# The halo of a causal convolution summed by ScalarE, and a ratio with two scalar factors, in a two-layer mLSTM and differential-attention trunk

## The chip, the core and the metric

The program runs on one core of a Trainium2 chip. The metric is device microseconds of one execution, as the median of three runs. In every text here PE is TensorE (PEld its weight loads), DVE is VectorE, ACT is ScalarE, POOL is GpSimd, and SP is the engine that issues the DMAs.

## What is computed

Two layers over 2048 positions of width 1024. Each layer normalises its input, multiplies it by one wide matrix, and gives the columns to four mLSTM heads and four differential-attention heads. The two places that the change touches are the causal convolution of the mLSTM's q and k columns, and the factor with which the second attention map is subtracted from the first:

```python
def causal_conv(x, w, b):          # w: 4 taps per channel
    y = lax.conv_general_dilated(x, w..., padding=[(K - 1, 0)], feature_group_count=C)
    return y + b
...
    qk = jax.nn.silu(causal_conv(jnp.concatenate([mq, mk], -1), conv_w, conv_b))
    mq_c, mk_c = jnp.split(qk, 2, axis=-1)
    hm = mlstm_chunkwise(to_heads(mq_c), to_heads(mk_c), to_heads(mv), mi + i_bias, mf + f_bias)
...
        p = jax.nn.softmax(jnp.where(mask, s, -jnp.inf), axis=-1)
        a = p[:, :, 0] - lam * p[:, :, 1]
        return jnp.einsum('bhqk,bhke->bhqe', a, vt)
```

## The kernel before, in words

Positions are cut into four time blocks of T = 512 (index `t`), heads into four units (`u`), each with one mLSTM head and one attention head. So there are 2 x 4 x 4 = 32 units of work. In each, PE projects the unit's columns: a group of 24 matmuls for one 128-column piece fills one PSUM tile `mm` (three buffers in all) with channels on the partitions and the 512 positions along the free dimension. Matrices are split into a high and a low part (`wh`, `wl`; `hth`, `htl`) and three products are summed. ACT makes `wh` from each loaded piece (L194), POOL makes `wl` (L196).

For the q piece and the k piece (`qk` = 0 and 1) the function `post` in `proj_conv` does the convolution; that is 64 convolutions in all. ACT writes the last tap and the bias into `cacc` (L406). DVE then adds three taps from PSUM, shifted by 1, 2 and 3 positions (L410). The first 1, 2 or 3 positions of a block need the last three positions of the block before it, the halo: a small tile of 128 x 3 kept from there. After each tap a second, small DVE instruction adds the halo's part of that tap (L412). Then ACT copies this block's last three positions into the halo tile (L414), and `silu2` follows: ACT's tanh of `cacc` (L394), and a DVE product (L395).

For attention, DVE takes the scores from PSUM into SBUF with their row maximum (L735), ACT takes the exponent with its sum (L679). When both maps of a query block are there, `ratio` sums the parts (`zz`, L687), takes the reciprocal of the second map's sum (L692) and multiplies it by the first map's sum and by `nl`, minus lambda (L693). `chunk` adds the second map, scaled by that, to the first (L699). PE transposes the result into `tpa`; ACT takes the high part of it (`ath`, L801), DVE the low part (`atl`, L802), and PE multiplies both with the values (`pv`). PE needs `ath` for the first of these products and `atl` for the second.

The code puts all this into one list of tasks with due times; each task emits its instructions, and a scheduler with a timeline of its own then sorts them into one queue for each engine. TensorE's tasks are held in the order of their streams by extra dependencies. So any change of an instruction can change the order of others in a queue. Each engine works through its queue in order.

Of the kernel before, what the change touches and what calls it, by code (L numbers as in the profile page):

```python
# [12 lines left out]
F32 = mybir.dt.float32  # L13
F32R = mybir.dt.float32r
BF16 = mybir.dt.bfloat16
AF = mybir.ActivationFunctionType
ALU = mybir.AluOpType
AX = mybir.AxisListType

P = 128  # L20
S = 2048
D = 1024
T = 512
# [29 lines left out]
def trunk_kernel(ctx, tc, x, w_ch, w_v0, w_v, w_o, nw, cw, cb, gb, mnw, msk, anw, lam,  # L53
                 fnw, rope, out, n_layers=NL, n_t=NT):
    nc = tc.nc
    V, A, G, PE, SY = nc.vector, nc.scalar, nc.gpsimd, nc.tensor, nc.sync

    cp = ctx.enter_context(tc.tile_pool(name="cp", bufs=1))
# [9 lines left out]
    def st(shape, tag, dt=F32, name=None):  # L68
        return sb.tile(shape, dt, tag=tag, name=name or tag, bufs=BUFS[tag])

    def sm(cols, name):
        return sb.tile([P, cols], F32, tag="s_" + name, name=name, bufs={"mx": 2, "zc": 2, "nm": 2, "s12": 4}.get(name, 1))
# [14 lines left out]
    def after(r, name):  # L87
        tc.add_manual_dep(r.ins, name, nosync, reason="TensorE order")
# [42 lines left out]
    def behind(r):  # L131

        if "r" in first:
            after(r, first["r"])
        return r

    def params(l):
        pr = par[l]
        for nm, src, w in (("cw", cw[l], 32), ("cb", cb[l], 8),
                           ("mnw", mnw[l], NH), ("msk", msk[l], NH), ("anw", anw[l], 1)):  # L140
            t_ = cp.tile([P, w], F32, tag=f"{nm}{l}", name=f"{nm}{l}")
            SY.dma_start(t_, src)
            pr[nm] = t_
        t_ = cp.tile([P, 8], F32, tag=f"gb{l}", name=f"gb{l}")
        SY.dma_start(t_, gb[l].partition_broadcast(P))
        pr["gb"] = t_
        lt = st([P, 4, 64], "tmp", name="lam")
        SY.dma_start(lt, lam[l].partition_broadcast(P))
        lam_init = 0.8 - 0.6 * math.exp(-0.3 * l)
        lp = st([P, 2, 64], "tmp", name="lp")  # L150
        behind(V.tensor_tensor(lp[:, 0], lt[:, 0], lt[:, 1], op=ALU.mult))
        behind(V.tensor_tensor(lp[:, 1], lt[:, 2], lt[:, 3], op=ALU.mult))
        ls = cp.tile([P, 4], F32, tag=f"ls{l}", name=f"ls{l}")
        V.tensor_reduce(out=ls[:, 0:2], in_=lp, axis=AX.X, op=ALU.add)
        A.activation(ls[:, 2:4], ls[:, 0:2], AF.Exp)
        nl = cp.tile([P, 1], F32, tag=f"nl{l}", name=f"nl{l}")

        V.tensor_tensor(nl, ls[:, 3:4], ls[:, 2:3], op=ALU.subtract)
        V.tensor_scalar(out=nl, in0=nl, scalar1=-lam_init, scalar2=None, op0=ALU.add)
        pr["nl"] = nl  # L160

        behind(V.tensor_scalar(out=pr["anw"], in0=pr["anw"], scalar1=(1.0 - lam_init), scalar2=0.5,
                               op0=ALU.mult, op1=ALU.mult))
        behind(V.tensor_scalar(out=pr["mnw"], in0=pr["mnw"], scalar1=0.5, scalar2=None, op0=ALU.mult))
        behind(V.tensor_scalar(out=pr["msk"], in0=pr["msk"], scalar1=0.25, scalar2=None, op0=ALU.mult))

        for h in range(NH):
            hq = cp.tile([P, 2, 3], F32, tag=f"halo{l}{h}", name=f"halo{l}{h}")
            G.memset(hq, 0.0)
            pr["halo"].append(hq)  # L170
        mc = cp.tile([1, NH], F32, tag=f"mc{l}", name=f"mc{l}")
        G.memset(mc, 0.0)
        pr["mc"] = mc
# [121 lines left out]
    def proj_ch(l, u, g, H, post):  # L295

        c = {}

        def hi(dc):
            def f():  # L300
                half, j = divmod(dc, 4)
                if dc == 0:
                    c["ps"] = pst("mm", [P, T])
                if j == 0:
                    c["w"] = load_w(w_ch[l, u, g, half], 512)
                w = c["w"][0][:, j * P:(j + 1) * P]
                mm(c["ps"], w, H["hh"][dc], dc == 0, False)
                mm(c["ps"], w, H["hl"][dc], False, False)
            return f

        def lo(d0):
            def f():
                for dc in (d0, d0 + 1):
                    j = dc % 4
                    mm(c["ps"], c["w"][1][:, j * P:(j + 1) * P], H["hh"][dc], False, dc == 7)
                if d0 == 6:
                    post(c["ps"])
            return f

        return [(0.44, f) for half in range(2)  # L320
                for f in [hi(4 * half + j) for j in range(4)] + [lo(4 * half + j) for j in (0, 2)]]
# [69 lines left out]
    def silu2(dst, src):  # L391

        th = st([P, T], "tmp", name="th")
        A.activation(th, src, AF.Tanh, scale=0.5)  # L394
        V.scalar_tensor_tensor(out=dst, in0=th, scalar=1.0, in1=src, op0=ALU.add, op1=ALU.mult)  # L395

    def proj_conv(l, u, qk, H, X):

        pr = par[l]

        def post(ps):
            halo = pr["halo"][u]
            ch = qk * NH + u
            w = lambda j: pr["cw"][:, ch * 4 + j:ch * 4 + j + 1]
            acc = st([P, T], "tmp", name="cacc")
            A.activation(acc, ps, AF.Identity, scale=w(3), bias=pr["cb"][:, ch:ch + 1])  # L406
            for j in (2, 1, 0):

                d = 3 - j
                V.scalar_tensor_tensor(out=acc[:, d:], in0=ps[:, 0:T - d], scalar=w(j), in1=acc[:, d:],  # L410
                                       op0=ALU.mult, op1=ALU.add)
                V.scalar_tensor_tensor(out=acc[:, 0:d], in0=halo[:, qk, j:3], scalar=w(j), in1=acc[:, 0:d],  # L412
                                       op0=ALU.mult, op1=ALU.add)
            A.activation(halo[:, qk], ps[:, T - 3:T], AF.Copy)  # L414
            nm = "mq" if qk == 0 else "mk"
            X[nm] = st([P, T], nm)
            silu2(X[nm], acc)

        return proj_ch(l, u, qk, H, post)
# [244 lines left out]
    def scores(l, t, u, X, pair):  # L664

        pr = par[l]
# [17 lines left out]
        def ratio(qi, cq, r=None):  # L684
            zz = X["zz"]
            qb = 2 * pair + qi
            z_ = V.tensor_reduce(out=zz[:, qb], in_=cq["zc"][:, :, 0:t + 1], axis=AX.X, op=ALU.add)  # L687
            if r is not None:
                after(z_, r)

            s_ = cq["s"] = sm(1, "s12")
            V.reciprocal(s_, zz[:, qb, 1:2])  # L692
            V.scalar_tensor_tensor(out=s_, in0=s_, scalar=zz[:, qb, 0:1], in1=pr["nl"], op0=ALU.mult, op1=ALU.mult)  # L693
            X["aa", pair].append(cq["pc"][0])

        def chunk(qi, cq, kt, r=None):
# [342 lines left out]
    if n_layers > 1:  # L1039
        at(60.0, lambda: params(1))  # L1040
    for k in range(-1, N + 1):
# [6 lines left out]
        if k >= 1:  # L1048
            Xp = Xs[k - 1]
            v1 = apply_v(*units[k - 1], Xp, 1)  # L1050
            a, d = v_rate[k - 1]
# [9 lines left out]
        segs = []  # L1061
        fetches = {}
        tm = None
        if cur:
            l, t, u = cur
            s = l * n_t + t
            H, X = Hs[s], Xs[k]
            q0, q1 = scores(l, t, u, X, 0), scores(l, t, u, X, 1)
            v0 = apply_v(l, t, u, X, 0)
            att += total(q0) + total(q1) + 1.1 * len(v0)  # L1070
            if u == 2 and s < last:
                at(xc, lambda s=s: rs0.__setitem__(s + 1, prep_x((s + 1) // n_t, (s + 1) % n_t)))
            segs.append((0.0, proj_conv(l, u, 0, H, X) + proj_conv(l, u, 1, H, X)))
            if u == 1 and s > 0:
                pl, pt_ = divmod(s - 1, n_t)
                segs.append((fin_t[k - 2] + 6.0, outproj(pl, pt_, 1, Xs[k - 3:k - 1])))
                if pl == n_layers - 1:
                    segs.append((0.0, [(0.0, lambda pl=pl, pt_=pt_: final(pl, pt_))]))
            segs.append((0.0, proj_gate(l, u, 2, H, X, "gzm")))
            segs.append((0.0, proj_gate(l, u, 3, H, X, "gza")))  # L1080
            if u == NH - 1 and s < last:
                op = outproj(l, t, 0, Xs[k - 3:k - 1])
                segs.append((fin_t[k - 2] + 6.0, op[:len(op) // 4]))

                pt = prep_t((s + 1) // n_t, (s + 1) % n_t, lambda s=s: rs0[s + 1], Hs[s + 1])
                segs.append((0.0, merge(pt, op[len(op) // 4:])))
                fetches[len(segs) - 1] = Hs[s + 1]
        elif k == -1:
            segs.append((0.0, prep_first(Hs[0])))
# [29 lines left out]
        if cur:  # L1119
            at(t0 + 0.01, load_k(l, t, u, X))  # L1120
            lat = 3.5 + 1.2 * (t + 1)
            d = (QF if k < N - 1 else QL) * dur / (len(q0) + len(q1))
# [26 lines left out]
    l, t = divmod(last, n_t)  # L1149
# [3 lines left out]
    op = outproj(l, t, 1, Xs[N - 2:N], (0, 1, 2), R, (0,), cw_)  # L1153
# [6 lines left out]
    op = outproj(l, t, 1, Xs[N - 2:N], (3,), R, (1,))  # L1160
# [89 lines left out]
```

## Time and profile before

| | us |
|---|---|
| median of three runs (2815.98, 2825.23, 2827.08) | 2825.23 |
| the profiled execution, its own time | 2837.46 |
| span of the profiled execution, from its first to its last instruction | 2835.5 |
| PE busy | 2671.6 (94%) |
| DVE busy | 1862.6 (66%) |
| ACT busy | 1649.2 (58%) |
| POOL busy | 1433.4 (51%) |
| mean granted clock of PE | 0.981 |

The profile is of one execution: for each engine it has every instruction with its start and duration, and for an idle stretch what ended it. The profiled execution took 0.4% more than the median of the runs; 2.0 us of its time lie outside the span.

### The profile page before, as it was taken

The page shows a single profiled execution, that of the slowest core. Times are in us where ns is not written, and L with a number is a line of the kernel's source. Part 1 is how long each engine was busy: PE and PEld are TensorE (multiplying, and loading weights), DVE is VectorE, ACT ScalarE, POOL GpSimd, SP SyncE. Part 2 cuts the span into 40 slices and gives each one's busy share as a digit, 9 for nine tenths or more (in the row PEclk, how much of TensorE's full clock was granted, in tenths as well). Part 3 has the DMA queues.
Part 4 walks back from the last instruction along what each step waited for, and adds up shares of the span by engine and source line. Part 5 has one row for each costly group of instructions (what it writes and reads, how often), then busy time and mean ns, then how long its engine had stood idle before and what let it go on. Part 6 is the DMA issues. An engine that isn't in the chain of part 4 may idle for free. (4 is left out here: it accounts for less than half of the span.)

```text
span 2835.5 us, 49306 instructions
## 1 busy us (share of the span) xinstructions
PE 2671.6 (94%) x16692; PEld 2371.3 (84%) x16692; DVE 1862.6 (66%) x4890; ACT 1649.2 (58%) x4413; POOL 1433.4 (51%) x1190
## 2 busy tenths in 40 slices
PE   7999899989999999999999999999999999998997
PEld 6898788888888888888888888888888888887887
DVE  5556565775767767567755566567667676776776
ACT  5555465565656556665555555555566555665665
POOL 5565655545454354344445656555554544445425
PEclk9999999999999999999999999999999999999999
DMA  6645555464544544434445455654557444464333
GB/s 203 174 131 157 169 167 149 140 200 150 167 144 128 173 127 127 131 108 139 147 142 177 141 169 154 198 188 137 159 145 231 141 138 154 116 192 145 100 104 119
DMA packets 249789, 431.02 MB, mean 152 GB/s; under 512 B 30400, under 2 KB 106688, under 8 KB 249536
## 3 DMA queue, kind: packets, MB, share of 16 engines
q1 hardware_dynamic: 249536, 427.87, 50.0%
q8 instruction: 132, 2.16, 0.3%
q14 instruction: 121, 0.99, 0.1%
HBM read 314.38 MB, written 63.05 MB: 133 GB/s over the span
## 5 line engine op out<-in xcount | busy, mean ns | idle before, releaser
L196 POOL TENSOR_TENSOR wl<-wr,wh 128x512 fp32r<-128x512 f32 (+1 forms) x684 | 907.6, 1332 | 1070.4 <-PE mm L106 461.7
L194 ACT ACTIVATE wh<-wr 128x512 fp32r<-128x512 f32 (+1 forms) x684 | 428.1, 628 | 414.2 <-PE mm L106 223.5
L106 PE MATMUL mm<-hth,wh 128*128 128x512 f32 x1536 | 619.7, 403 | 0.4 <-ACT vaug L347 0.4
L106 PE MATMUL mm<-htl,wh 128*128 128x512 f32 x1536 | 610.3, 397 | 0.0
L735 DVE TENSOR_SCALAR_CACHE_REDUCE p<-sc 128x512 f32<-128x512 f32 (+3 forms) x640 | 384.7, 606 | 141.7 <-PE sc L106 116.8
L679 ACT ACTIVATE p<-p,nm 128x512 f32<-128x512 f32 (+3 forms) x640 | 413.8, 649 | 97.6 <-DVE nm L675 86.9
L106 PE MATMUL mm<-hth,wl 128*128 128x512 f32 x1536 | 438.8, 400 | 0.0
L106 PEld LDWEIGHTS mm<-hth,wh 128*128 128x128 f32 x1536 | 291.2, 190 | 60.2 <-ACT vaug L347 1.2
L106 PEld LDWEIGHTS mm<-htl,wh 128*128 128x128 f32 x1536 | 291.0, 189 | 56.8
L106 PEld LDWEIGHTS mm<-hth,wl 128*128 128x128 f32 x1536 | 284.1, 190 | 60.2
L699 DVE SCALAR_TENSOR_TENSOR p<-p,s 128x512 f32<-128x512 f32 (+2 forms) x320 | 284.9, 901 | 1.8
L106 PE MATMUL mm<-wh,hth 128*128 128x256 f32 (+1 forms) x1024 | 268.2, 291 | 16.9 <-DVE gt L349 6.0
L802 DVE TENSOR_TENSOR atl<-tpa,ath 128x512 fp32r<-128x512 f32 x288 | 197.1, 684 | 120.4 <-ACT ath L801 119.4
L106 PE MATMUL mm<-wh,htl 128*128 128x256 f32 (+1 forms) x1024 | 264.2, 288 | 0.0
L106 PE MATMUL sc<-kp,q 128*128 128x512 f32 x768 | 246.2, 406 | 5.5 <-DVE p L735 5.4
L801 ACT ACTIVATE ath<-tpa 128x512 fp32r<-128x512 f32 x288 | 170.1, 591 | 139.7 <-PE tpa L109 134.2
L106 PEld LDWEIGHTS mm<-wh,hth 128*128 128x128 f32 x1024 | 198.4, 194 | 22.3 <-issue 9.0
L106 PEld LDWEIGHTS mm<-wh,htl 128*128 128x128 f32 x1024 | 198.3, 194 | 2.5
L109 PE MATMUL tpa<-ident,p 128*128 128x128 f32 x1088 | 186.1, 276 | 15.1 <-DVE tpa L794 8.7
L410 DVE SCALAR_TENSOR_TENSOR cacc<-mm,cw,cacc 128x511 f32<-128x511 f32 (+2 forms) x192 | 141.6, 737 | 66.5 <-ACT cacc L406 64.7
L106 PE MATMUL pv<-ath,vp 128*128 128x256 f32 x768 | 178.9, 287 | 1.1 <-ACT ath L801 1.1
L106 PE MATMUL mm<-wl,hth 128*128 128x256 f32 (+1 forms) x1024 | 166.8, 292 | 0.4 <-POOL wl L196 0.4
(211 smaller groups left out, 5685.1 us busy)
## 6 DMA issues: line engine op xcount, KB each, us to landing
wr<-in_w_ch_dram SPq DMA_DIRECT2D x384, 256.0 KB, 2.7
wr<-in_w_o_dram SPq DMA_DIRECT2D x140, 256.0 KB, 2.9
q<-ab SPq DMA_DIRECT2D x256, 128.0 KB, 2.4
vp<-vd SPq DMA_DIRECT2D x48, 512.0 KB, 4.6
wr<-in_w_v_dram SPq DMA_DIRECT2D x96, 256.0 KB, 3.7
kp<-kd SPq DMA_DIRECT2D x48, 512.0 KB, 3.8
wr<-in_w_v_dram SPq DMA_DIRECT2D x64, 264.0 KB, 3.0
kc<-ab SPq DMA_DIRECT2D x256, 64.0 KB, 2.0
```

What stands on the lines that cost most here:

```text
L106: pin(PE.matmul(o, l, r, start=start, stop=stop, skip_group_check=True))
L109: pin(PE.transpose(o, i, ident[:n, :n]))
L194: A.activation(wh[:, :n], wr[:, :n], AF.Copy)
L196: G.tensor_tensor(wl[:, :n], wr[:, :n], f32(wh[:, :n]), op=ALU.subtract)
L410: V.scalar_tensor_tensor(out=acc[:, d:], in0=ps[:, 0:T - d], scalar=w(j), in1=acc[:, d:], op0=ALU.mult, op1=ALU.add)
L679: A.activation(pp[:, :w], pp[:, :w], AF.Exp, bias=nm[:, m:m + 1], accum_out=zc[:, m, kt:kt + 1])
L699: d_ = V.scalar_tensor_tensor(out=pc[0][kt][:, :w], in0=pc[1][kt][:, :w], scalar=cq["s"][:, 0:1], in1=pc[0][kt][:, :w], op0=ALU.mult, op1= ...
L735: ev = V.tensor_scalar(out=pp[:, :w], in0=ps[:, :w], scalar1=0.125, scalar2=None, op0=ALU.mult, op1=ALU.max, accum_out=c["mx"][:, m, kt:kt ...
L801: A.activation(ah, p2, AF.Copy)
L802: lo_ = V.tensor_tensor(al, p2, f32(ah), op=ALU.subtract)
```

## The change

Two edits. First, the halo. The tile now holds, for q and k, two places of three columns that the time blocks use in turn, and what it keeps is no longer the last three values but the sums that the next block needs from them: ACT writes the last three values times the weight of the farthest tap (L416), and then adds the nearer taps' parts, one column at a time, with three more instructions (L419), each with a per-partition scale and a per-partition bias. The next block adds the three sums to `cacc` with one DVE instruction (L412 of the new file) behind the three taps. The first time block has no halo to add, and the last one none to leave. Both layers use one tile for a unit's halo, and the memset is gone. Second, the ratio: one instruction with a tensor operand and a scalar becomes one with two scalar operands.

```diff
         for h in range(NH):
-            hq = cp.tile([P, 2, 3], F32, tag=f"halo{l}{h}", name=f"halo{l}{h}")
-            G.memset(hq, 0.0)
+            hq = cp.tile([P, 2, 2, 3], F32, tag=f"halo{h}", name=f"halo{l}{h}")
             pr["halo"].append(hq)
...
-            halo = pr["halo"][u]
...
+            was, left = [pr["halo"][u][:, qk, i] for i in (t % 2, 1 - t % 2)]
             acc = st([P, T], "tmp", name="cacc")
             A.activation(acc, ps, AF.Identity, scale=w(3), bias=pr["cb"][:, ch:ch + 1])
             for j in (2, 1, 0):
...
                 V.scalar_tensor_tensor(out=acc[:, d:], in0=ps[:, 0:T - d], scalar=w(j), in1=acc[:, d:],
                                        op0=ALU.mult, op1=ALU.add)
-                V.scalar_tensor_tensor(out=acc[:, 0:d], in0=halo[:, qk, j:3], scalar=w(j), in1=acc[:, 0:d],
-                                       op0=ALU.mult, op1=ALU.add)
-            A.activation(halo[:, qk], ps[:, T - 3:T], AF.Copy)
+            if t > 0:
+                V.tensor_tensor(acc[:, 0:3], acc[:, 0:3], was, op=ALU.add)
+            if t < n_t - 1:
+
+                e = ps[:, T - 3:T]
+                A.activation(left, e, AF.Copy, scale=w(0))
+                for j in (1, 2):
+                    for i in range(3 - j):
+                        A.activation(left[:, i:i + 1], e[:, i + j:i + j + 1], AF.Identity, scale=w(j), bias=left[:, i:i + 1])
...
             V.reciprocal(s_, zz[:, qb, 1:2])
-            V.scalar_tensor_tensor(out=s_, in0=s_, scalar=zz[:, qb, 0:1], in1=pr["nl"], op0=ALU.mult, op1=ALU.mult)
+            V.tensor_scalar(out=s_, in0=s_, scalar1=zz[:, qb, 0:1], scalar2=pr["nl"][:, 0:1], op0=ALU.mult, op1=ALU.mult)
```

How the queues move is seen at two places. The first is DVE's queue at the q convolution of layer 0, t = 3, u = 1. Before:

```order
L410 SCALAR_TENSOR_TENSOR cacc<-mm,cw_265,cacc 128x511
L412 SCALAR_TENSOR_TENSOR cacc<-halo_293,cw_265,cacc 128x1
L410 SCALAR_TENSOR_TENSOR cacc<-mm,cw_265,cacc 128x510
L412 SCALAR_TENSOR_TENSOR cacc<-halo_293,cw_265,cacc 128x2
L410 SCALAR_TENSOR_TENSOR cacc<-mm,cw_265,cacc 128x509
L412 SCALAR_TENSOR_TENSOR cacc<-halo_293,cw_265,cacc 128x3
L687 TENSOR_REDUCE zz<-zc 128x2
L692 RECIPROCAL s_13491<-zz 128x1
L835 TENSOR_TENSOR ar<-zz 128x4
L693 SCALAR_TENSOR_TENSOR s_13491<-s_13491,zz,nl_285 128x1
L802 TENSOR_TENSOR atl<-tpa,ath 128x512
```

And of the change, the same place (its lines are numbered a little differently: L409 are the taps, L412 the sum of the halo, L698 the ratio, L807 makes `atl`):

```order
L409 SCALAR_TENSOR_TENSOR cacc<-mm,cw_265,cacc 128x511
L409 SCALAR_TENSOR_TENSOR cacc<-mm,cw_265,cacc 128x510
L409 SCALAR_TENSOR_TENSOR cacc<-mm,cw_265,cacc 128x509
L412 TENSOR_TENSOR cacc<-cacc,halo_292 128x3
L692 TENSOR_REDUCE zz<-zc 128x2
L697 RECIPROCAL s_13493<-zz 128x1
L840 TENSOR_TENSOR ar<-zz 128x4
L698 TENSOR_SCALAR s_13493<-s_13493,zz,nl_285 128x1
L807 TENSOR_TENSOR atl<-tpa,ath 128x512
```

In front of `atl`, for which PE waits, three small instructions became one behind the taps, and the ratio has changed its form; the rest stands as it stood.

The second is ACT's queue at the k convolution of layer 0, t = 2, u = 1. Before:

```order
L406 ACTIVATE cacc<-mm,cb_267,cw_265 128x512
L801 ACTIVATE ath<-tpa 128x512
L636 ACTIVATE yhm<-ytm 128x512
L194 ACTIVATE wh<-wr 128x512
L573 ACTIVATE ytm<-mq,msk_271 128x512
L414 ACTIVATE halo_293<-mm 128x3
L394 ACTIVATE th<-cacc 128x512
L801 ACTIVATE ath<-tpa 128x512
L194 ACTIVATE wh<-wr 128x512
```

And of the change (L405 begins `cacc`, L416 and L419 write the halo, L393 is the tanh, L806 makes `ath`, L193 `wh`):

```order
L405 ACTIVATE cacc<-mm,cb_267,cw_265 128x512
L806 ACTIVATE ath<-tpa 128x512
L641 ACTIVATE yhm<-ytm 128x512
L193 ACTIVATE wh<-wr 128x512
L416 ACTIVATE halo_292<-mm,cw_265 128x3
L393 ACTIVATE th<-cacc 128x512
L578 ACTIVATE ytm<-mq,msk_271 128x512
L419 ACTIVATE halo_292<-mm,halo_292,cw_265 128x1 x2
L806 ACTIVATE ath<-tpa 128x512
L930 ACTIVATE oj,sq_98<-xr 128x256
L193 ACTIVATE wh<-wr 128x512
L419 ACTIVATE halo_292<-mm,halo_292,cw_265 128x1
```

The copy of the halo still stands between the taps and the tanh; three instructions follow it behind the tanh, here with other work between them, and the PSUM tile `mm` is free only after the last. In the program of the change L416 waits for the third tap, and the tanh for the sum of the halo; before, L414 waited for the third small DVE instruction, and the tanh stood behind it without a wait of its own on DVE.

## Rows read from the trace of the kernel before

**Rows 1.** The head of the page: busy time of each engine, share of the span, instructions; and the clock granted to PE in tenths, in 40 slices.

```profile
PE 2671.6 (94%) x16692; PEld 2371.3 (84%) x16692; DVE 1862.6 (66%) x4890; ACT 1649.2 (58%) x4413; POOL 1433.4 (51%) x1190
PEclk9999999999999999999999999999999999999999
```

**Rows 2.** The waits of PE: the waiting instruction, what ended the wait, us in total, times, the longest. The list has 31 rows; the first three, five of the next, and the last.

```profile
PE pv L106 <- DVE atl L802: 35.2, 34, 4.6
PE mm L109 <- DVE x L247: 12.4, 4, 7.1
PE ml L109 <- ACT hs L617: 10.5, 7, 4.7
...
PE ml L106 <- ACT kw L586: 10.1, 9, 2.1
...
PE pv L106 <- ACT ath L801: 8.6, 9, 2.7
...
PE mm L106 <- ACT halo L414: 1.5, 1, 1.5
...
PE tpa L109 <- DVE gza L848: 0.2, 1, 0.2
```

**Rows 3.** DVE's instructions by line: what is written and read, shapes, count | busy us in all, mean ns of one | idle time before them and who ended it.

```profile
L699 DVE SCALAR_TENSOR_TENSOR p<-p,s 128x512 f32<-128x512 f32 (+2 forms) x320 | 284.9, 901 | 1.8
...
L410 DVE SCALAR_TENSOR_TENSOR cacc<-mm,cw,cacc 128x511 f32<-128x511 f32 (+2 forms) x192 | 141.6, 737 | 66.5 <-ACT cacc L406 64.7 <-ACT mp L528 1.5
L412 DVE SCALAR_TENSOR_TENSOR cacc<-halo,cw,cacc 128x1 f32<-128x1 f32 (+2 forms) x192 | 99.2, 517 | 0.0
...
L693 DVE SCALAR_TENSOR_TENSOR s<-s,zz,nl 128x1 f32<-128x1 f32 x128 | 45.8, 358 | 2.1
...
L692 DVE RECIPROCAL s<-zz 128x1 f32<-128x1 f32 x128 | 20.3, 159 | 2.0
```

**Rows 4.** All engines in order of time at the first convolution: start us, duration us, engine, line, instruction. The rows of DVE and POOL.

```profile
58.67 1.34 POOL L446 TENSOR_TENSOR t<-t,ra 128x512 f32<-128x512 f32 x1
...
59.58 0.45 DVE L412 SCALAR_TENSOR_TENSOR cacc<-halo,cw,cacc 128x1 f32<-128x1 f32 x1
...
59.97 1.30 POOL L196 TENSOR_TENSOR wl<-wr,wh 128x512 fp32r<-128x512 f32 x1
...
60.61 0.68 DVE L412 SCALAR_TENSOR_TENSOR cacc<-halo,cw,cacc 128x2 f32<-128x2 f32 x1
...
61.23 1.28 POOL L452 TENSOR_TENSOR ab<-t,ab 128x512 fp32r<-128x512 f32 x1
...
61.87 0.66 DVE L412 SCALAR_TENSOR_TENSOR cacc<-halo,cw,cacc 128x3 f32<-128x3 f32 x1
```

**Rows 5.** Single lines of DVE: count, shortest/median/longest ns of one, when the first and the last start, shapes.

```profile
L412 DVE SCALAR_TENSOR_TENSOR cacc<-halo,cw,cacc x192: 197/417/4593, 59.6 to 2721.7; 128x1 f32<-128x1 f32 x64, 128x2 f32<-128x2 f32 x64, 128x3 f32<-128x3 f32 x64
L212 DVE TENSOR_SCALAR xrs<-xrs x16: 145/154/156, 5.6 to 628.6; 128x1 f32<-128x1 f32 x16
L836 DVE TENSOR_SCALAR ass<-ass x31: 150/170/1328, 139.7 to 2744.1; 128x4 f32<-128x4 f32 x31
```

**Rows 6.** ACT's instructions by line, columns as in group 3. L586 reads PSUM with a per-partition scale, L596 reads as much of PSUM without one; L528 is the smallest read of PSUM.

```profile
L586 ACT ACTIVATE kw<-ml,cols 128x128 f32<-128x128 f32 x128 | 45.9, 359 | 69.5 <-DVE st L584 69.2
...
L596 ACT ACTIVATE hs<-ml 128x129 f32<-128x129 f32 x128 | 34.5, 270 | 46.6 <-PE ml L106 45.9
...
L414 ACT ACTIVATE halo<-mm 128x3 f32<-128x3 f32 x64 | 10.8, 169 | 85.0 <-DVE cacc L412 84.8
...
L528 ACT ACTIVATE mp<-ml 16x1 f32<-16x1 f32 x8 | 1.1, 143 | 0.0
```

**Rows 7.** The waits of all engines, the row of the halo's copy: us in total, times, the longest.

```profile
ACT halo L414 <- DVE cacc L412: 84.8, 44, 4.4
```

**Rows 8.** All engines in order of time around 1105 us, layer 0, t = 3, u = 1, the place of DVE's queue shown above. In brackets the idle time of the engine before, and who ended it.

```profile
1102.14 1.42 DVE L412 SCALAR_TENSOR_TENSOR cacc<-halo,cw,cacc 128x1 f32<-128x1 f32 x1
...
1102.24 1.30 POOL L196 TENSOR_TENSOR wl<-wr,wh 128x512 fp32r<-128x512 f32 x1
...
1104.15 0.20 DVE L412 SCALAR_TENSOR_TENSOR cacc<-halo,cw,cacc 128x2 f32<-128x2 f32 x1
...
1104.88 0.39 PE L106 MATMUL pv<-ath,vc 128*128 128x256 f32 x1 [1.62 <-ACT ath L801]
...
1105.43 1.26 POOL L196 TENSOR_TENSOR wl<-wr,wh 128x512 fp32r<-128x512 f32 x1 [1.88 <-ACT halo L414]
1105.44 1.26 DVE L693 SCALAR_TENSOR_TENSOR s<-s,zz,nl 128x1 f32<-128x1 f32 x1
1106.63 0.68 DVE L802 TENSOR_TENSOR atl<-tpa,ath 128x512 fp32r<-128x512 f32 x1
...
1107.36 0.58 PE L106 MATMUL pv<-atl,vc 128*128 128x256 f32 x1 [2.09 <-DVE atl L802]
```

**Rows 9.** Two stretches: start:end us, length, busy us of PE, PEld, DVE, ACT and POOL (with counts), PE's granted clock, DMA share, GB/s.

```profile
1105.80:1112.40 6.60, 5.04 (x15) 4.26 (x16) 3.43 (x5) 1.87 (x4) 2.17 (x2) 0.50 0.70 173
...
2611.00:2614.20 3.20, 3.19 (x12) 3.00 (x13) 0.18 (x1) 0.99 (x3) 0.48 (x1) 0.50 0.41 149
```

**Rows 10.** PE in order of time: the first of 44 waits of PE behind which L412 or L693 stands in the chain.

```profile
352.84 0.30 PE L109 MATMUL ml<-ident,stk 96*128 96x96 f32 x1 [1.03 <-ACT stk L537]
```

**Rows 11.** The same view, the last of these 44 waits.

```profile
2775.94 0.39 PE L106 MATMUL pv<-atl,vc 128*128 128x256 f32 x1 [0.39 <-DVE atl L802]
```

More of the change, by code (lines that the diff above doesn't have):

```diff
@@ L395, in silu2, with proj_conv @@
         V.scalar_tensor_tensor(out=dst, in0=th, scalar=1.0, in1=src, op0=ALU.add, op1=ALU.mult)
-    def proj_conv(l, u, qk, H, X):
+    def proj_conv(l, t, u, qk, H, X):
         pr = par[l]
         def post(ps):
-            halo = pr["halo"][u]
             ch = qk * NH + u
             w = lambda j: pr["cw"][:, ch * 4 + j:ch * 4 + j + 1]
+            was, left = [pr["halo"][u][:, qk, i] for i in (t % 2, 1 - t % 2)]
             acc = st([P, T], "tmp", name="cacc")
@@ L1072, in trunk_kernel @@
                 at(xc, lambda s=s: rs0.__setitem__(s + 1, prep_x((s + 1) // n_t, (s + 1) % n_t)))
-            segs.append((0.0, proj_conv(l, u, 0, H, X) + proj_conv(l, u, 1, H, X)))
+            segs.append((0.0, proj_conv(l, t, u, 0, H, X) + proj_conv(l, t, u, 1, H, X)))
             if u == 1 and s > 0:
```

## The prediction

> **What bounds the kernel now.** The head of the page first: PE is busy for 94% of the span, DVE for 66%, ACT 58%, POOL 51% [rows 1]. PE has the work that must be done; the others cost time only where PE waits for them. PE's 2671.6 us of the 2835.5 leave 164 us idle. The list of PE's waits comes next: of its 31 rows those that end with DVE add up to 106 us, ACT's to 39, POOL's to 8; the longest by far is `pv` waiting for `atl`, the second half of the evacuation of the transposed probabilities, 35.2 us in 34 waits [rows 2]. No single cause dominates: some 130 waits of a little over a microsecond, at places where DVE's or ACT's queue is late. So the change is worth what it shortens in front of those places. A long wait costs more than itself: behind the one at 1105 us PE worked at half its clock (0.50, the 1.2 GHz level) for 6.6 us, and behind one that ended at 2611 for 3.2 us [rows 9].
>
> **What the small DVE instructions cost.** 192 of L412 take 99.2 us, 517 ns each, though they write one to three columns; 128 of L693 take 45.8 us, 358 ns each, for one column [rows 3]. The shortest L412 takes 197 ns [rows 5]. The rest is a wait that the view books as work: at the first convolution the three L412 end at 60.03, 61.29 and 62.53 us, and three POOL instructions end at 60.01, 61.27 and 62.51 [rows 4]. A DVE instruction with two operands from SBUF stands still until POOL's running one is done, with DVE's queue behind it. The taps (L410, one operand from PSUM) take 737 ns [rows 3] and don't show this. L693 has two tensor operands, too: at 1105.44 it starts beside a POOL instruction of 1105.43 and both take 1.26 us [rows 8].
>
> **The change part by part.**
>
> *DVE, the halo.* 99.2 us go. 48 additions come; two SBUF operands, so they can wait for POOL. Bounds: 0.20 us (the shortest L412) and 0.60 us (somewhat over the mean). I take the mean, 0.52: 48 x 0.52 = 25 us. Saved: 74 us (70 to 90).
>
> *DVE, the ratio.* The new form has one tensor operand; its scalars are columns. No row has it with two scalars from memory. Nearest: L692, one column in and out, 128 times, 159 ns in the mean [rows 3], and L212, the same operation on one column with constants, at most 156 ns in 16 [rows 5]. I take 0.16: 128 x 0.16 = 20 us, saved 25. The other bound is 0.36 as before, nothing saved.
>
> The Trainium skill's page "VectorE: DVE Perf Modes", section "What auto-detection actually checks", lets an operation with one source use both SBUF ports when source and destination lie in SBUF with even or equal outermost sizes; by it the new ratio would still meet POOL there, and the saving of 25 us would go. Of the trace's one-source operations L836, four columns wide, does wait (up to 1328 ns, median 170), as that rule has it; L212, one column wide like the ratio, never does [rows 5]. I go by the row of one column.
>
> Together DVE loses 145 - 45 = 100 us, 5% of its work. Some of the ratio's wait is passed on: the scaled addition (L699) often stands right behind it, has two SBUF operands, and already takes 901 ns in the mean [rows 3].
>
> *ACT.* 64 copies of 169 ns go (10.8 us). 48 L416 come, PSUM in, with a scale, and 144 L419 on one column with scale and bias. A scale costs 359 - 270 = 0.09 us (L586 against L596), the smallest PSUM read is 0.143 (L528) [rows 6]. So L416 is 0.17 + 0.09 = 0.26, L419 is 0.14 + 2 x 0.09 = 0.32: 12 + 46 - 11 = +48 us. Lower bound, if scalars cost nothing on one column: 48 x 0.17 + 144 x 0.143 - 11 = +18. Against that stands a wait: the halo's copy waits 84.8 us for DVE in 44 of 64 cases, 1.9 us each [rows 7]. Its new form waits for the third tap alone, which comes three small instructions (1.55 us) earlier; of 1.9 us some 0.5 stay, so 60 us of waiting go. The tanh now waits for the halo's sum, 0.52 us behind the third tap, of which L416 covers 0.26: 48 x 0.26 = 12 us return. ACT's queue is thus as late as before on the whole: 60 - 12 of waiting against 48 of work. Queued behind L416 and the tanh are `wh`, `ath` and the mLSTM's copies. On PE's waits for ACT (39 us) I put 3 us of loss, since the 20 convolutions without a wait only pay.
>
> *PSUM.* `mm` is free after the last L419 instead of L414, at worst some microseconds later. PE waited for L414 once, 1.5 us [rows 2]; three buffers cover the rest. Memsets and tile names: nothing, POOL is half idle.
>
> *PE.* I followed each of PE's 129 waits over 0.2 us (152 us) back through the queues. Behind 44 of them (46 us) L412 or L693 stands in the chain, the first at 352 us and the last at 2776 us [rows 10, 11]. Crediting each with its small instructions' whole time, at most the wait's length, gives 25 us. The place at 1105 us shows how: `ath` is there at 1104.9, but `atl` starts at 1106.63, behind 1.42 + 0.20 us of L412 and 1.26 of L693, and PE waits 2.09 us [rows 8]. In the new queue `atl` can follow `ath` at once. Since 100 of the 145 us go, 25 x 100/145 = 17 us. The two stretches at half clock [rows 9] lie behind such waits; they cost half of 9.8 us, and I count 3 us. From these 20 us I take a third off, because a PE that arrives earlier meets the next late thing: 14; less ACT's 3: **11 us**.
>
> The profiled execution took 2837.5 us (2.0 outside its span), so it would take 2826.5. It is 12 us above the median of the runs, 2825.2; on that median, **2814 us**.
>
> **The rivals.**
>
> *The gain doesn't arrive: 2825 us.* DVE's freed time is slack, or POOL's hold is met by the next two-operand instruction instead. For it: DVE idles a third of the span, and L699 stands ready to inherit the wait. Against it: in front of `atl` stands no L699 at the place shown. The weaker form, the ratio still waiting for POOL and each addition at 0.60, saves 145 - 46 - 29 = 70 us on DVE: 25 x 70/145 = 12, with the clock 15, two thirds of it 10, less ACT's 3 leaves 7 us: 2818.
>
> *ACT becomes late: 2846 us.* Behind each of 48 tanhs stand three L419, 0.96 us, ahead of `ath`, `wh` or `kw`. If three quarters of these 46 us land on PE, 35 - 14 = +21 us: 2846. It decides as soon as more than 14 us land (no gain left), and is slower by over 0.5% from 28. Against it: ACT's queue starts that stretch earlier by about as much, and ACT idles 42%.
>
> *The new order gains or loses by itself.* Queues are sorted anew, and PE's waits belong in part to the order; with 129 of them at 1.2 us, redrawing some moves the sum by perhaps 10 to 15 us either way. With the mechanism's gain and the clock: 2795.
>
> **How the numbers follow.** 0.5% is 14 us, about what a measurement of this kernel can tell from no change: under 2811 is faster, over 2839 slower. The forecast (gain of 5 to 20 us, 2805 to 2820) gets 0.50; no arrival (2820 to 2832) 0.20; a larger gain by the order 0.16; ACT late, or an order that loses, 0.14. Of the forecast's case somewhat over two fifths lie under 2811: faster 0.22 + 0.16 = 0.38. Slower: four fifths of the last case, 0.11. Same: the rest, 0.51. The range that leaves out two in ten reaches into both outer cases: 2797 to 2837; the likeliest's own is 2805 to 2820.
>
> **What would show it.** DVE's busy time near 1763 us; the halo's sum 48 times at 0.2 to 0.6 us; the ratio at 0.16 us without long ones (its longest under 0.25). ACT busy 18 to 48 us more, L419 at 0.14 to 0.32 us; the wait of the halo's write for DVE near 25 us instead of 84.8, and the tanh with a new one. PE's idle time from 164 to about 150 us, its row `pv` for `atl` shorter, the wait at the place of 1105 us gone. Wrong it would be if PE's waits for `atl` stay while DVE's work falls, or if waits of PE for `wh`, `ath` or `kw` grow by 20 us.

## The result, and the profile after the change

The change takes 2806.64 us (median of 5 runs, 2804.09 to 2811.82) against 2825.23 us (5 runs, 2815.98 to 2827.08): a ratio of 0.9942, 95% interval 0.9924 to 0.9960, 16 us faster by the ratio. The forecast was 2814 us, "same" the likeliest sign and "faster" the next; the time lies inside the range, 7 us below the forecast. The ratio lies just on the faster side of 0.5%, with an interval that reaches over it, so of the signs it is the second likeliest that came, and barely. The profiled run is 2806.64 us, at its median; that of before was 12 us above its own, so about 12 of the 31 us between the two traces are chance.

The head of the page, to be read against [rows 1]:

```profile
PE 2657.6 (95%) x16692; PEld 2360.0 (84%) x16692; DVE 1796.2 (64%) x4746; ACT 1689.2 (60%) x4541; POOL 1439.6 (51%) x1182
```

DVE lost 66.4 us, ACT gained 40.0, POOL 6. PE's own busy time fell by 14 us although it runs the same 16692 matmuls: in this execution the mean granted clock was 0.987, in that of before 0.981. That is a difference of two single executions; how the clock stands in all of them comes with the experiments.

DVE's changed instructions by line, columns as in [rows 3] (line numbers are those of the changed kernel: L409 are the taps, L412 the halo's sum, L698 the ratio, L704 the scaled addition):

```profile
L704 DVE SCALAR_TENSOR_TENSOR p<-p,s 128x512 f32<-128x512 f32 (+2 forms) x320 | 280.3, 887 | 1.7
L409 DVE SCALAR_TENSOR_TENSOR cacc<-mm,cw,cacc 128x511 f32<-128x511 f32 (+2 forms) x192 | 142.9, 744 | 74.7 <-ACT cacc L405 68.3 <-ACT mp L533 2.9
L698 DVE TENSOR_SCALAR s<-s,zz,nl 128x1 f32<-128x1 f32 x128 | 34.2, 267 | 2.2
...
L412 DVE TENSOR_TENSOR cacc<-cacc,halo 128x3 f32<-128x3 f32 x48 | 23.3, 486 | 0.0
```

The same two lines singly, shortest/median/longest, as in [rows 5]:

```profile
L698 DVE TENSOR_SCALAR s<-s,zz,nl x128: 157/272/276, 81.1 to 2745.3; 128x1 f32<-128x1 f32 x128
...
L412 DVE TENSOR_TENSOR cacc<-cacc,halo x48: 140/324/1293, 338.1 to 2691.7; 128x3 f32<-128x3 f32 x48
```

The halo costs 23.3 us instead of 99.2, the ratio 34.2 instead of 45.8. The sum still meets POOL (longest 1293 ns); the ratio never does (longest 276 ns in 128), but its median is 272.

ACT, columns as in [rows 6]: L419 are the nearer parts, L393 the tanh, L416 the first part of the sum left to the next block.

```profile
L419 ACT ACTIVATE halo<-mm,halo,cw 128x1 f32<-128x1 f32 x144 | 42.8, 345 | 0.1
L393 ACT ACTIVATE th<-cacc 128x512 f32<-128x512 f32 x64 | 40.1, 626 | 12.5 <-DVE cacc L412 12.3
...
L416 ACT ACTIVATE halo<-mm,cw 128x3 f32<-128x3 f32 x48 | 12.4, 258 | 18.2 <-DVE cacc L409 18.0
```

The copy's wait for DVE, 84.8 us in [rows 7], is 18.0 here, and the tanh has the new one, 12.3.

PE's waits, four of 31 rows, against [rows 2]:

```profile
PE pv L106 <- DVE atl L807: 30.9, 34, 3.6
...
PE pv L106 <- ACT ath L806: 10.8, 11, 2.7
PE ml L106 <- ACT kw L591: 8.2, 7, 1.8
...
PE ml L109 <- ACT hs L622: 7.5, 4, 4.9
```

The rows that end with DVE add up to 97 us (106 before, 101 in grouped below), ACT's to 30.5 (39, 43), POOL's to 8 (8, 6). No wait for `ath`, `kw` or `hs` grew by more than 2.2 us.

Last, the place of [rows 8], now at 1096 us, in order of time, DVE and PE:

```profile
1093.83 2.32 DVE L409 SCALAR_TENSOR_TENSOR cacc<-mm,cw,cacc 128x511 f32<-128x511 f32 x3
...
1096.06 0.15 DVE L412 TENSOR_TENSOR cacc<-cacc,halo 128x3 f32<-128x3 f32 x1
...
1097.14 0.27 DVE L698 TENSOR_SCALAR s<-s,zz,nl 128x1 f32<-128x1 f32 x1
...
1097.24 0.39 PE L106 MATMUL pv<-ath,vc 128*128 128x256 f32 x1 [1.65 <-ACT ath L806]
1097.33 0.68 DVE L807 TENSOR_TENSOR atl<-tpa,ath 128x512 fp32r<-128x512 f32 x1
...
1098.06 0.39 PE L106 MATMUL pv<-atl,vc 128*128 128x256 f32 x1 [0.43 <-DVE atl L807]
```

`atl` follows `ath` at once, and PE's wait of 2.09 us is 0.43. That looks like the mechanism at the place where it was foretold, but it doesn't show it: in *grouped* below, which runs the queues of before, the same wait is 0.38 us. Whether the mechanism made the time is a question for the experiments, also because the whole program's queues were sorted anew.

### The profile page after: what moved, and what is told of

It is laid out like the page before. It is cut to its first block, busy times and chain, and to the rows that moved or that the text cites. A ratio compares the mean times of both kernels' runs of the same rounds, so it can differ in the third digit from the quotient of the medians.

```text
span 2804.9 us, 49271 instructions
## 1 busy us (share of the span) xinstructions
PE 2657.6 (95%) x16692; PEld 2360.0 (84%) x16692; DVE 1796.2 (64%) x4746; ACT 1689.2 (60%) x4541; POOL 1439.6 (51%) x1182
## 5 line engine op out<-in xcount | busy, mean ns | idle before, releaser
L193 ACT ACTIVATE wh<-wr 128x512 fp32r<-128x512 f32 (+1 forms) x684 | 428.7, 628 | 406.4 <-PE mm L106 209.2
L807 DVE TENSOR_TENSOR atl<-tpa,ath 128x512 fp32r<-128x512 f32 x288 | 197.1, 684 | 134.5 <-ACT ath L806 133.2
L704 DVE SCALAR_TENSOR_TENSOR p<-p,s 128x512 f32<-128x512 f32 (+2 forms) x320 | 280.3, 887 | 1.7
L806 ACT ACTIVATE ath<-tpa 128x512 fp32r<-128x512 f32 x288 | 170.2, 591 | 147.6 <-PE tpa L109 137.3
L409 DVE SCALAR_TENSOR_TENSOR cacc<-mm,cw,cacc 128x511 f32<-128x511 f32 (+2 forms) x192 | 142.9, 744 | 74.7 <-ACT cacc L405 68.3
```

Of the source, the lines that this page charges most:

```text
L193: A.activation(wh[:, :n], wr[:, :n], AF.Copy)
L704: d_ = V.scalar_tensor_tensor(out=pc[0][kt][:, :w], in0=pc[1][kt][:, :w], scalar=cq["s"][:, 0:1], in1=pc[0][kt][:, :w], op0=ALU.mult, op1= ...
L806: A.activation(ah, p2, AF.Copy)
L807: lo_ = V.tensor_tensor(al, p2, f32(ah), op=ALU.subtract)
```

## Experiments

**First: each edit alone, and the change with less work.** One theory was that the time follows DVE's shorter queue, part by part; the other, that the new order of the queues makes it.

*halo_only*: the halo edit, with the ratio as it was; the queues are what the scheduler then makes of it.

```
-            V.tensor_scalar(out=s_, in0=s_, scalar1=zz[:, qb, 0:1], scalar2=pr["nl"][:, 0:1], op0=ALU.mult, op1=ALU.mult)
+            V.scalar_tensor_tensor(out=s_, in0=s_, scalar=zz[:, qb, 0:1], in1=pr["nl"], op0=ALU.mult, op1=ALU.mult)
```

> The halo's edit alone, the ratio in its old form. Theory 1 (DVE's shorter queue in front of PE's waits): the halo took 74 of the 100 us that DVE was to lose, so about three quarters of the change's gain of 16 us: 0.9958 of before, DVE's busy time some 55 to 75 us less, and PE's idle time and the stretches at half clock between those of before and of the change. Theory 2 (the gain is that of a luckier order): no relation to the share of the work; anywhere from 0.990 to 1.005.

Measured: 2826.08 us, ratio 1.0003 (0.9989 to 1.0017).

*ratio_only*: the other half, the same two lines exchanged in the kernel before.

> The ratio's edit alone, the halo as before. Theory 1: DVE loses what the ratio lost in the change, 45.8 - 34.2 = 12 us, about an eighth of the work, so 2 to 4 us of time: 0.999. Theory 2: anywhere from 0.990 to 1.005; the sum of the two edits' effects needn't be that of the change.

Measured: 2824.25 us, 1.0000 (0.9986 to 1.0014).

*grouped*: before, with the three small halo instructions moved behind the third tap in the source.

```
+            for j in (2, 1, 0):
+                d = 3 - j
                 V.scalar_tensor_tensor(out=acc[:, 0:d], in0=halo[:, qk, j:3], scalar=w(j), in1=acc[:, 0:d],
```

> The kernel before, with the three small DVE instructions of a convolution behind its three taps instead of between them: same instructions, another order. Theory 1: DVE's work stays, within 3 us of before (0.999 to 1.001), DVE's busy time within 20 us of 1863. Theory 2: the order alone moves the time by as much as the change did, more than 8 us either way (below 0.997 or above 1.003).

Measured: 2826.89 us, 1.0008 (0.9993 to 1.0023). But the edit moved nothing: the scheduler put each small instruction back behind its tap, and in the traces all five queues are those of before, instruction for instruction. So this is the kernel before once more, and says nothing of the order. It does show how far two executions of the same queues lie apart. The head of its page, and the place of [rows 8] in it (L414 are the small halo instructions, L695 the ratio, L804 makes `atl`), in order of time, DVE, POOL and PE:

```profile
PE 2666.0 (94%) x16692; PEld 2365.5 (84%) x16692; DVE 1873.2 (66%) x4890; ACT 1650.2 (58%) x4413; POOL 1431.5 (51%) x1190
```

```profile
1096.70 0.21 DVE L414 SCALAR_TENSOR_TENSOR cacc<-halo,cw,cacc 128x1 f32<-128x1 f32 x1
1096.80 1.28 POOL L196 TENSOR_TENSOR wl<-wr,wh 128x512 fp32r<-128x512 f32 x1
1096.83 0.74 DVE L410 SCALAR_TENSOR_TENSOR cacc<-mm,cw,cacc 128x510 f32<-128x510 f32 x1
1097.49 0.62 DVE L414 SCALAR_TENSOR_TENSOR cacc<-halo,cw,cacc 128x2 f32<-128x2 f32 x1
...
1099.34 0.22 DVE L695 SCALAR_TENSOR_TENSOR s<-s,zz,nl 128x1 f32<-128x1 f32 x1
...
1099.48 0.68 DVE L804 TENSOR_TENSOR atl<-tpa,ath 128x512 fp32r<-128x512 f32 x1
...
1100.22 0.54 PE L106 MATMUL pv<-atl,vc 128*128 128x256 f32 x1 [0.38 <-DVE atl L804]
```

DVE's busy time is 1873.2 us here and 1862.6 in before's trace, with the same instructions in the same order. At the place POOL's instructions happen to stand otherwise: the first small instruction takes 0.21 us and not 1.42, the second 0.62 and not 0.20 (POOL's running one ends at 1098.08, and it at 1098.11), and the ratio 0.22 and not 1.26. The wait of 2.09 us that the prediction took as its example was chance in one execution.

*no_near*: the change without the nearer parts.

```
-                for j in (1, 2):
-                    for i in range(3 - j):
-                        A.activation(left[:, i:i + 1], e[:, i + j:i + j + 1], AF.Identity, scale=w(j), bias=left[:, i:i + 1])
```

> The changed kernel without the three L419 (the nearer taps' parts of the halo are left out, so the first positions of a block are summed without them). It takes 43 us of ACT's work away from behind the tanh and frees the PSUM tile earlier. Theory 1 counted 3 us for ACT's work: 0.993 of before, within 4 us of the change. Rival (ACT's tail costs PE): 10 us or more under the change, 0.990 or less, with PE's waits for ath, kw and wh shorter by as much.

Measured: 2814.72 us, 0.9960 (0.9944 to 0.9975): less work than the change, and no faster than it.

Neither edit alone gained anything, although DVE's busy time fell by 31 us in halo_only (1831.8) and by 21 in ratio_only (1841.8). Read like that, the work is worth nothing and the order everything. But each of these kernels except grouped has queues of its own, so work and order were never separated.

**Second: the work and the order taken apart.** A list at the end of the file gives the order of each engine's instructions, taken from another kernel, and each instruction is tied to the one ahead of it on its engine, without a wait. All five queues are then those of the list, and the traces show them so (the texts of what was expected call such an order a row):

```
+    made = {i.name: i for i in nc.cur_bb.bb.instructions}
...
+        for p_, n_ in zip(names, names[1:]):
...
+                tc.add_manual_dep(made[n_], p_, nosync, reason="queue order")
```

*before_neworder*: before's work in the change's order.

> The work of the kernel before, instruction for instruction, but every engine's queue fixed to the row of the change: each small halo op stands behind its tap, the halo's copy where the sum's first ScalarE op stands, everything else where the change has it. Theory 'order' (the gain is the place of the neighbours in the queues, not the removed work): 0.994 to 0.997 of before, 2808 to 2817 us, time at half clock below 95 us. Theory 'work' (the gain is DVE's 66 us, and the order does nothing): 1.000, 2825 us. Theory 'both together': 0.998 to 1.000.

Measured: 2831.74 us, 1.0029 (1.0012 to 1.0046). The new order by itself loses, which none of the three theories had. The largest row of its list of PE's waits:

```profile
PE pv L106 <- DVE atl L802: 41.4, 38, 4.7
```

It was 35.2 in [rows 2] (32.9 in grouped), and is 30.9 with the change's work in this order.

*after_oldorder*: the change's work in before's order.

> The work of the change, but every engine's queue fixed to the row of the kernel before (the sum of the halo where the third small op stood, the sum's first ScalarE op where the copy stood, the three nearer parts right behind the tanh that followed it). Theory 'order': 0.999 to 1.001 of before, 2822 to 2828 us. Theory 'work': 0.993 to 0.996, 2805 to 2814 us. 'Both together': 0.998 to 1.000.

Measured: 2802.47 us, 0.9926 (0.9905 to 0.9947). The whole gain is there without the new order.

*halo_neworder*: the halo edit alone, in the change's order.

> The halo edit alone (the ratio as before), which by itself stood at 1.000, with every queue fixed to the row of the change. Theory 'order': 0.994 to 0.996, as the change. Theory 'work': between the halo edit alone and the change by the ratio's share of DVE's time (10 of 66 us), 0.999. If the ratio's POOL wait is what counts: 1.000.

Measured: 2813.06 us, 0.9960 (0.9948 to 0.9972). The work that gained nothing in its own order gains 0.4% against before in this one, and 0.7% against before's work in the same order.

*after_haloorder*: the change's work in the order of halo_only.

> The work of the change in the row of the halo edit alone, which stood at 1.000. Theory 'order': 0.999 to 1.001. Theory 'work': 0.994 to 0.995, as the change.

Measured: 2821.35 us, 0.9984 (0.9969 to 0.9999). This order takes back three quarters of the gain.

These last two results alone would have fitted the order theory, the second roughly. The two before them don't: with before's work the change's order loses, and the change's work gains without it.

The theory that the order makes the gain falls, and so does the reading of halo_only as "no gain": that kernel's gain was eaten by its own order. One place where that order loses can be seen. Waits of all engines in after_haloorder:

```profile
ACT bc L572 <- DMA bc<-bw: 66.3, 27, 5.7
...
PE ml L109 <- ACT hs L622: 15.9, 6, 5.5
```

and the same rows of halo_neworder, which has the better order:

```profile
ACT bc L572 <- DMA bc<-bw: 54.3, 25, 6.0
...
PE ml L109 <- ACT hs L622: 8.1, 4, 5.2
```

The place, in order of time in after_haloorder: SP issues the transfer of `bc`, ACT waits for it, `hs` stands behind, PE waits for `hs`:

```profile
1142.70 0.36 SPq L563 DMA_DIRECT2D bc<-bw  x1
...
1149.83 0.40 ACT L572 ACTIVATE bc<-bc,cols 128x128 f32<-128x128 f32 x1 [3.98 <-DMA bc<-bw]
...
1154.74 0.69 ACT L622 ACTIVATE hs<-hs,den 128x128 f32<-128x128 f32 x2
...
1155.18 0.77 PE L109 MATMUL ml<-ident,hs 128*128 128x128 f32 x2 [5.49 <-ACT hs L622]
```

In this order ACT comes to `bc` before its data is there, and `hs` stands behind it. In the change `bc` also stands ahead of `hs`, but ACT comes to it later and doesn't wait; the same `hs` come no earlier, at 1157.05, but PE has other matmuls standing ahead of their transposes and waits 1.05 us. The stretch 1145 to 1165 us, columns as in [rows 9], first in after_haloorder and then in the change:

```profile
1145.00:1165.00 20.00, 11.06 (x39) 8.19 (x39) 5.30 (x16) 9.29 (x30) 8.98 (x8) 0.67 0.32 82
```

```profile
1145.00:1165.00 20.00, 16.80 (x86) 13.10 (x85) 8.33 (x23) 12.67 (x43) 11.07 (x12) 1.00 0.40 126
```

39 matmuls against 86 in 20 us, at a mean clock of 0.67 against 1.00. Over these 20 us PE is busy for 5.7 us less, and runs part of the rest at the half clock; the whole price of this order against the change's, by the ratios, is 12 us. That this one place makes most of it is not shown.

**Third: what the work consists of, all in before's order.**

*halo_oldorder*: the halo edit alone.

> The halo edit alone (the ratio as before), every queue in the row of the kernel before. 'Sum' theory (each edit's work and each row of the queues has a price of its own, and they add): the ratio edit was worth 0.0018 in either row where both were run (0.9960 to 0.9942, 1.0003 to 0.9984), so 0.9926 + 0.0018 = 0.9944, 2808 us. 'Only together' theory (the halo edit gains nothing without the ratio edit in the row of before): 1.000.

Measured: 2814.19 us, 0.9963 (0.9951 to 0.9975): nearer to the sum's 0.9944 than to 1.000, but the interval leaves out both.

*padded_oldorder*: the change, with the small DVE instructions put back as ballast.

```
+                if j > 0 or t == 0:
+                    V.scalar_tensor_tensor(out=left[:, 0:d], in0=pr["cw"][:, j:3], scalar=w(j), in1=acc[:, 0:d],
+                                           op0=ALU.mult, op1=ALU.add)
```

> The change in the row of the kernel before, with DVE's instructions put back as ballast: behind each of the first two taps (in the first block of a layer behind all three) an instruction of the old form, two operands from SBUF and one to three columns, that writes to the halo slot which ScalarE overwrites next. DVE has 192 small instructions again, ScalarE has the change's work. 'DVE' theory (the gain is DVE's shorter queue): the halo's 0.7% is gone, 0.997 to 0.999, 2816 to 2822 us, and the half-clock time is back above 95 us. 'ScalarE' theory (the gain is that ScalarE no longer waits 60 us for the last small instruction ahead of the halo's copy and the tanh): 0.993 to 0.995.

Measured: 2828.36 us, 1.0012 (0.9998 to 1.0026): the whole gain is gone. That is a longer time than either theory had, since the ratio edit is still in this kernel; why its 0.4% (see the table below) went too is not shown. The ballast by line, and the head of the page:

```profile
L412 DVE SCALAR_TENSOR_TENSOR halo<-cw,cacc 128x1 f32<-128x1 f32 (+1 forms) x144 | 79.2, 550 | 0.0
```

```profile
PE 2670.3 (94%) x16692; PEld 2370.8 (84%) x16692; DVE 1857.1 (66%) x4890; ACT 1686.1 (60%) x4541; POOL 1430.7 (51%) x1182
```

and after_oldorder's:

```profile
PE 2658.6 (95%) x16692; PEld 2362.8 (84%) x16692; DVE 1809.9 (65%) x4746; ACT 1688.2 (60%) x4541; POOL 1436.5 (51%) x1182
```

In instructions the two differ in DVE's 144 alone, 47 us of DVE's busy time, and every other instruction stands in the same order. ACT's work is equal, but its wait for DVE ahead of L416's counterpart is back as well (59.9 us against 20.4). Of these 59.9 us 27.7 end with the ballast itself, which writes the tile that ACT writes next, in the first time block of a layer, where it stands behind the third tap; the other 32.2 end with the third tap. So the ballast delays DVE, and it delays what ACT takes from DVE; this run doesn't tell the two apart.

*no_near_oldorder*: the change without the nearer parts (edit as no_near).

> The change in the row of the kernel before without the three nearer parts on ScalarE (144 of L419, 43 us); it leaves out the parts of the halo that the second and third last columns give. If ScalarE's added work is hidden: as the change in that row, 0.991 to 0.993. If it costs the 3 us of my sum: 0.9915. If it costs half of itself: 0.985.

Measured: 2803.65 us, 0.9926 (0.9904 to 0.9948). The head of its page:

```profile
PE 2663.0 (95%) x16692; PEld 2366.0 (84%) x16692; DVE 1805.6 (64%) x4746; ACT 1654.8 (59%) x4397; POOL 1436.8 (51%) x1182
```

ACT has 33 us less, and the time is that of after_oldorder. No price of ACT's added work is seen, as far as the two intervals can tell (0.3%, 8 us).

*dve_left_oldorder*: the nearer parts on DVE.

```
-                    for i in range(3 - j):
-                        A.activation(left[:, i:i + 1], e[:, i + j:i + j + 1], AF.Identity, scale=w(j), bias=left[:, i:i + 1])
+                    V.scalar_tensor_tensor(out=left[:, 0:3 - j], in0=e[:, j:3], scalar=w(j), in1=left[:, 0:3 - j],
+                                           op0=ALU.mult, op1=ALU.add)
```

> The change in the row of the kernel before, but the nearer parts are summed by DVE (two instructions of two columns and one, one operand from PSUM, behind the mq or mk instruction) in place of ScalarE's three. DVE gets 96 instructions, some 20 us, ScalarE loses 43. If DVE's queue sets the price at 0.3 us a microsecond and ScalarE's work is hidden: 6 us more than the change in that row, 0.9947. If ScalarE's work costs as much as DVE's: 6 us less, 0.990.

Measured: 2809.37 us, 0.9946 (0.9926 to 0.9966). DVE has 14 us more than in after_oldorder (1824.0), ACT 32 us less (1655.8), and the time is not shorter; its centre lies where DVE's price put it, but the two intervals overlap.

All that was measured of work and order, as ratios to before:

| work \ order of the queues | before's | the change's | halo_only's |
|---|---|---|---|
| before's | 1.0000 | 1.0029 | not run |
| halo edit | 0.9963 | 0.9960 | 1.0003 |
| both edits | 0.9926 | 0.9942 | 0.9984 |

Down a column only the work changes, along a row only the order. The halo edit is worth 0.4% in before's order and 0.7% in the change's; the ratio edit 0.4, 0.2 and 0.2%. Each step has an uncertainty of 0.2 to 0.3%. Going from the change's order to halo_only's costs 0.4% with either work. The work and the order add roughly (the halo edit's two values lie 0.3% apart, a little more than their uncertainty), and the order's part is as large as an edit's.

The granted clock sheds light on the order's part. The same table with the mean granted clock over all executions of each kernel (83 of before, 5 to 12 of each other):

| work \ order of the queues | before's | the change's | halo_only's |
|---|---|---|---|
| before's | 0.986 | 0.982 | not run |
| halo edit | 0.986 | 0.984 | 0.982 |
| both edits | 0.987 | 0.985 | 0.983 |

In before's order these three works have the same clock; in the other two orders it is lower. The clock has two levels, 1 and 0.5 (2.4 and 1.2 GHz), so twice the missing share of the span is time at the half clock: 78, 81 and 74 us down the first column, 101, 90 and 83 down the second, 99 and 93 down the third. Half of such a difference is the most that it can have cost. As an estimate that is up to 12 us where the change's order lost 8 with before's work, and up to 9 and 10 us where halo_only's lost 11 and 16 against before's. A good part of an order's price may thus be the clock; whether the clock makes it or follows from PE's waits is not shown.

No kernel was shown to beat the change: after_oldorder's 0.9926 and the change's 0.9942 have overlapping intervals.

## Why the prediction was right, and which steps were not

The time lies where the text put it, and the cause is the one that it named: in before's order the change's work gains without any change of order (after_oldorder), and 144 small DVE instructions put back take the gain away (padded_oldorder). How much of it is PE waiting for DVE, and how much for ACT behind DVE, is open. And the sum reached its 11 us by errors that point in opposite directions, so that it came within 7 us is in part luck.

**DVE loses 100 us: too much, 66.** The additions were right (25 us said, 23.3 measured). The ratio's 0.16 us was the mis-sized term: it takes 0.267, so 34.2 us and not 20. What it was to be free of, POOL, it is free of. The prediction read the page "VectorE: DVE Perf Modes" of the Trainium skill, section "What auto-detection actually checks", as letting it meet POOL; the rule there is on the outermost size that is not one, and a single column has none, so it needn't reach this operation. No instruction of 128 was longer than 276 ns, while POOL's run for 1.3 us through half of the span. What is left is 0.11 us over L692 and L212, one column without scalars from memory [rows 3, 5]; the two scalars are its likely cause, though no run takes them away by themselves.

The other part of the gap is how rows are added. By rows, DVE lost 145.0 - 23.3 - 34.2 = 87.5 us; its busy time, which counts overlapping time once, fell by 66.4 (by 77.0 from grouped's trace). At the place above the three taps begin at 1093.83 and end at 1096.15, and the sum begins at 1096.06: neighbouring rows overlap. Summed one by one, DVE's rows are 2107.9 us before and 2018.9 after, the busy times 1862.6 and 1796.2: 245.3 and 222.7 us lie double. With the 144 instructions fewer 22.6 us of double time went, 0.16 us for each, which was never time of the queue. Little was passed on: all DVE rows together lost 89.0 us where the changed ones lost 87.5, and the scaled addition (L704), named as the likeliest heir, takes 887 ns against 901 [rows 3]. The heirs were DVE's products behind the tanh: `mq` takes 915 ns in the mean against 797 before (796 in grouped), `mk` 782 against 699 (698), together 6 us.

**ACT: right.** +48 us said, +40 measured; L416 at 0.26 (0.258), L419 at 0.32 (0.345), the remaining wait "near 25" (18.0), the tanh's new one 12 (12.3). The Trainium skill's page "ScalarE: Activation LUTs", section "What ACT_TABLE_LOAD costs", gives 93 ns for each per-partition operand; L416 and L419 differ by 87 ns with one such operand more, in agreement. The loss of 3 us that was put on PE is not seen: without L419 the time is the same, to 8 us. The rival in which ACT becomes late, at a cost of 35 us, falls with that.

**PE gains 14 us from DVE: too little per microsecond.** This is the step that was off. The credit was 25 us on 145 of DVE's, 0.17 for each. In before's order 0.74% or 21 us came with 53 us less of DVE's busy time (1862.6 to 1809.9; 63 from grouped's), 0.3 to 0.4 for each; against padded_oldorder it is 24 us on 47.

The small term was PE's waits. PE's idle time is 163.9 us before, 160.6 in grouped and 160.5 in padded_oldorder, and 143.9 in after_oldorder: 17 to 20 us less, where two thirds of 17 were counted. From padded_oldorder to after_oldorder the waits that end with DVE fell by 7.7 us (97.9 to 90.2) and those that end with ACT by 8.4 (42.4 to 34.0). Taking a third off, because the next late thing would come, was a guess in the wrong direction. The walk back from each wait was of one execution, too: the wait that it gave as example, at 1105 us and followed by 6.6 us at the half clock, is as short in grouped (0.38 us) and padded_oldorder (0.44) as in the change (0.43). That it went was thus no sign of the mechanism.

The clock gave less than the profiles say. The mean granted clock of the profiled execution of padded_oldorder and then of after_oldorder:

```profile
core 0: 2830.8 us, clock 0.982
```

```profile
core 0: 2802.5 us, clock 0.988
```

That is 102 us at the half clock and 67, and PE's busy time fell by 11.7 us (2670.3 to 2658.6) for the same matmuls. But over all executions the means are 0.984 (12 of padded_oldorder) and 0.987 (6 of after_oldorder), 89 us and 74, and before's is 0.986. Against padded_oldorder the clock can have given some 7 us; against before it gave next to nothing, so the 3 us that the text counted for it are not seen.

**The order: real, and of the size given.** The text let a new order move the time by 10 to 15 us either way. The change's order costs 8 us with before's work (1.0029). Halo_only's costs 12 us more than the change's with either work. So 21 us of gain became 16, though with the change's work the loss against before's order, 0.0016, is within the uncertainty.

In short: 100 us instead of 53 to 66, times 0.17 instead of 0.3 to 0.4, is about as much as was measured, and a small loss by order took the place of ACT's. That the two errors nearly cancel is luck.

**The rival "the gain doesn't arrive"** looked true in halo_only and ratio_only. For the first, the same work in two other orders shows that it was its order. For ratio_only the order was not isolated, and it stays open whether its 21 us of DVE time were eaten in the same way; its mean clock, 0.984 in 12 executions against 0.986 in the 32 of before beside them, lies where the other new orders have it. Open, too, is how much of the gain is PE waiting for DVE itself and how much for ACT behind DVE; no kernel kept one and removed the other.

## What to carry to other kernels

Where a scheduler sorts queues anew after every edit, an edit tried alone measures its work and a new order together; put both works into the same fixed order before an edit is called useless. Look in the trace whether the queue has moved as the edit meant it; here one edit's had not. Such a second trace of the same queues is worth having, since it tells which waits at a place are chance. Count a queue's gain by busy time and not by the sum of its rows, and judge the clock by all executions and not by the profiled one. Here PE returned 0.3 to 0.5 us for each microsecond of DVE's busy time, where waits walked back in one trace credited 0.17. Small instructions of one engine that wait for another engine's running instruction were worth moving to an engine that idles, though each takes longer there than at its shortest here.

## What the runs showed of the hardware beyond that

- A DVE operation on one column with two scalars from memory takes 0.267 us in the mean (157 to 276 ns), 0.11 more than one-column operations without; it was never held by POOL in 128 cases, while the sum of two operands from SBUF, three columns, took up to 1293 ns.
- DVE's instructions overlap their neighbours in the trace, by 0.05 us in the mean (245.3 us over 4890 rows before).
- Two executions of the same queues (before and grouped) kept DVE busy for 1862.6 and 1873.2 us; the ratio at the place of [rows 8] took 1.26 us beside a POOL instruction of 1.26, and 0.22 with none beside it.
- The same 16692 matmuls kept PE busy for 2657.6 us in the change and for 2673.4 in ratio_only, with mean granted clocks of 0.987 and 0.981.
